# A chunked WKV kernel: six pairs loaded ahead, column sums in four column tiles of TensorE, and their copies on VectorE

## The chip, the core and the metric

The kernel runs on one core of a Trainium2 chip. The metric is the device time of one execution in microseconds (us). Every number below comes from runs of this kernel or from one profiled execution of it.

## The reference

The inputs are k and v of shape (16, 2048, 256), and two vectors w and u of 256. For each batch and channel a recurrence runs over the 2048 time steps. Cut to what matters:

```python
for t in range(seq_len):
    kk, vv = k[b, t], v[b, t]
    ww = u + kk
    qq = maximum(pp, ww)
    e1, e2 = exp(pp - qq), exp(ww - qq)
    output[b, t] = (e1 * aa + e2 * vv) / (e1 * bb + e2 + 1e-08)
    ww = pp - w + kk
    qq = maximum(ww, kk)
    e1, e2 = exp(ww - qq), exp(kk - qq)
    aa, bb, pp = e1 * aa + e2 * vv, e1 * bb + e2, qq
```

So an output is a weighted mean of the earlier v, with weights that are exponentials of k and of the distance in time, plus a weight with u for the current step.

## The kernel before, in words

**Tiling.** Time is cut into a head of 32 steps and 16 chunks ("steps", c = 0 to 15) of 126. Time lies on the partitions. The unit of work is a pair: 126 time rows of four batches, held as two tiles of 512 columns (two batches by 256 channels each). A step has four pairs. With the two pairs of the head (placed as pairs 2 and 3) there are 66 pairs.

**What is done with a pair n.**
- `load` (L111) brings k into a tile `kr` (float32) and v into `vr` (converted to bfloat16 by the transfer). `AHEAD` buffers of each exist, and the loop loads pair n + AHEAD in slot n. The k of pairs 0 and 1 and of the head is issued on SyncE's queue, all else on GpSimd's, which also writes the outputs.
- `round_k` (L283, VectorE) casts k into `km`. `logs` (L292, TensorE) makes the logarithms of two sets of weights by four matmuls with the matrices `NLE` and `NLZ` into PSUM `X`. From pair 8 on there is one `X`, of four banks.
- `exps` (L313, ScalarE) takes the exponentials of `X` into `ez` (bfloat16). `times_v` (L324, VectorE) multiplies them by v into the other half of `ez`.
- `sums` (L348, TensorE) adds up the weights and the weighted v over each half of the chunk: four matmuls of 512 columns with the one-hot matrices `OHE` and `OHV` (48 columns wide), all accumulated over the four pairs of a step into one PSUM tile `tot` of 48 rows.
- Ten slots later `den` and `num` (L500, L521, TensorE) form denominators and numerators, four matmuls each. `log_den` and `invert` (L509, L516, ScalarE) take Ln and Exp(-x), `mult` (L531, VectorE) multiplies, and `store` writes the output. PSUM holds one buffer of two banks for `den` and one of one bank for `num`.

**What is done once a step.** `copy_sums` (L366, ScalarE) copies `tot` into `ts`; `turn_sums` (L371, TensorE) transposes it by four matmuls with `Ir`; `split_sums` (VectorE) copies the result into `tsum`. Some 15 tiny operations on VectorE and ScalarE (`state_*`, `inject_*`, `carr*`) carry the state to the next step; `turn_carries` transposes it, and `inject` copies it to `row` and sends it by SyncE's DMAs into two rows of `ez`.

**The order.** `K` (L35) pins the order of each engine to the order of the program text, so the loop at L613 is the schedule. Slot n runs, in text order: load; `a3`; exps(n); `d0`; round_k(n+1); `p0`; num of tile 0 of pair n-12; `d1`; `a0`; `p1`; invert of pair n-11; `a2`; den and log_den of pair n-10; mult of tile 0; `d2`; `d3`; logs(n+1); num of tile 1; `p3`; times_v(n); sums(n); `p2`; `d4`; mult of tile 1 and store; `d5`; `p4`; `a1`. Each name in code marks is a place for small work. `PLANS` (L571) puts each small function in a place of a slot, counted from the last pair of its step: "steady" for c = 1 to 13, "before" for 14, "last" for 15.

In the steady plan `copy_sums` stands in slot 1 at `a0`, right after exps; the second half of the state (`state_add` 1 and `state_decay` 1) stands in slot 5 at `d2` and `d4`, after `inject` at `d0`. Slot 5 of a step is slot 1 of the next.

Of the kernel before, what the change touches and what calls it, by code (L numbers as in the profile page):

```python
# [22 lines left out]
def kernel(  # L23
# [35 lines left out]
    NH = NG * GB  # L59
    AHEAD = 4  # L60
    LAG = 10
    HALVES = 8
    RS = 2.0 ** -43
# [32 lines left out]
    def is_head(n):  # L96
        return pairs[n][0] < 0
# [5 lines left out]
    def tiles_of(n):  # L103
        return 1 if pairs[n] == (-1, 1) else 2
# [6 lines left out]
    def load(n):  # L111
        kr = kpool.tile([128, 4, Dm], F32, tag="kr", name="kr")
        vr = vpool.tile([128, 4, Dm], BF16, tag="vr", name="vr")
        kr_of[n], vr_of[n] = kr, vr
        c, p = pairs[n]
        if is_head(n):
            if p == 1:
                K(POOL.memset(kr[64:96, 0:2, :], 0.0))
                K(POOL.memset(vr[64:96, 0:2, :], 0.0))
            for t, x, eng in ((kr, k, SP), (vr, v, POOL)):  # L120
                for g in range(NG):
                    b = 6 * g + 4 * p
                    e = min(b + 2 * tiles_of(n), B)
                    if b < e:
                        K(eng.dma_start(out=t[g * GB:(g + 1) * GB, 0:e - b, :],  # L125
                                        in_=x[b:e, 0:T0, :].rearrange("n t d -> t n d")))
        else:
            t0 = T0 + c * TC
            r = min(128, T - t0)
            K((SP if n < 2 else POOL).dma_start(  # L130
                out=kr[0:r, :, :], in_=k[4 * p:4 * p + 4, t0:t0 + r, :].rearrange("n t d -> t n d")))
            if n >= 2:
                load_v(n)


    def load_v(n):
        c, p = pairs[n]
# [19 lines left out]
    def matrix(name, dt, width=128):  # L157
        return consts.tile([128, width], dt, tag=name, name=name)
# [10 lines left out]
    Ir = consts.tile([48, 48], F32R, tag="Ir", name="Ir")  # L169
# [31 lines left out]
    def step_matrices(E, Z, rows, N, io):  # L201
# [15 lines left out]
    OHE, OHV, OHhE, OHhV = [matrix(x, BF16, 56) for x in ("OHE", "OHV", "OHhE", "OHhV")]  # L217

    unit(0, NH)
    unit(1, NH + 1)  # L220
# [3 lines left out]
    K(POOL.memset(OHhV, 0.0))  # L224
    for g in range(NG):
        K(POOL.memset(OHhE[g * GB:(g + 1) * GB, 8 + 3 * g:9 + 3 * g], 1.0))
        K(POOL.memset(OHhV[g * GB:(g + 1) * GB, 24 + 3 * g:25 + 3 * g], 1.0))
        select(OHhE[:, 40 + 3 * g:41 + 3 * g], NE, 1.0, NH + g, -1, 1, 0)
    for n in range(2, AHEAD):
        load(n)  # L230
    kms = [consts.tile([128, 4, Dm], F32R, tag=f"km{j}", name=f"km{j}") for j in range(2)]
    for t in kms:
        K(SC.activation(t[96:128, :, :], row_of(96, 128), ACT.Copy))
# [3 lines left out]
        K(SC.activation(t[96:98, :, :], row_of(96, 98), ACT.Copy))  # L237

    def matrices_for_sums():
        K(DVE.tensor_copy(Ir, I1[0:48, 0:48]))  # L240
        for t, x in ((OHE, 8), (OHV, 24)):
            fill(t, 0.0)
            fill(t[0:HS, x:x + 1], 1.0)
            K(DVE.tensor_single_scalar(t[:, x + 8:x + 9], cc[:, 4:5], 2.0, op=ALU.mult))
        K(DVE.tensor_copy(OHE[:, 40:49:8], cc[:, 2:4]))

    def matrices_for_head():
        step_matrices(NLEh, NLZh, 0, NH, IOh)
# [60 lines left out]
    def ez_of(n):  # L309
        j = 2 * (n % 2)  # L310
        return EZ[n // 2][:, :, j:j + tiles_of(n), :]
# [20 lines left out]

    TOT, SUMS = {}, {}

    def step_of(n):
# [10 lines left out]
    def sums(n):  # L348
        c = step_of(n)
        head = c < 0  # L350
        if n == first_of[c]:
            TOT[c] = psn.tile([128, D], F32, tag="num", name="num")[0:48] if head else pst.tile(
                [48, D], F32, tag="tot", name="tot")
# [12 lines left out]
    def copy_sums(c):  # L366
        ts = small.tile([48, D], F32R, tag="ts", name="ts")
        K(SC.activation(ts, TOT.pop(c), ACT.Copy))  # L368
        st[c, "ts"] = ts

    def turn_sums(c):  # L371
# [192 lines left out]
    def at(slot, where, f, *args):  # L564
        later.setdefault((slot, where), []).append((f, args))

    def small_work(n, where):
        for f, args in later.pop((n, where), []):
# [135 lines left out]
```

## Time and profile before

| what | value |
|---|---|
| median of 4 runs | 298.59 us (297.81 to 299.89) |
| the profiled execution's own time | 297.94 us |
| its span, first to last instruction | 296.2 us |
| TensorE busy | 267.5 us (90%) |
| ScalarE busy | 270.0 us (91%) |
| VectorE busy | 247.7 us (84%) |
| GpSimd busy | 161.6 us (55%) |
| granted TensorE clock | 0.99 |

The profiled execution took 1.7 us more than its span, and it lies 0.65 us under the median. Three engines are busy most of the time, so the shares alone do not say which one sets the pace; that has to be read slot by slot. From about 66 us to 247 us the slots repeat with a period of four.

### The profile page before, as it was taken

How to read it: one execution, taken by the hardware profiler on the slowest of the kernel's cores; microseconds unless marked ns; L12 is line 12 of the kernel's file. 1: busy time of each engine (PE TensorE's matmuls, PEld its weight loads, DVE VectorE, ACT ScalarE, POOL GpSimd, SP SyncE). 2: the span in 40 equal slices, each digit the busy share in tenths (PEclk: the TensorE clock that was granted, in tenths of full speed). 3: DMA queues.
4: the chain of work that ended last, by engine and by line, in shares of the span. 5: the costliest groups of instructions: out<-in, count | busy, mean ns of one | idle time of the engine just before them, and what ended most of it. 6: DMA issues, size and time to landing. Idle time of an engine off the chain costs nothing.

```text
span 296.2 us, 3949 instructions
## 1 busy us (share of the span) xinstructions
PE 267.5 (90%) x1132; PEld 123.9 (42%) x1132; DVE 247.7 (84%) x501; ACT 270.0 (91%) x312; POOL 161.6 (55%) x231
## 2 busy tenths in 40 slices
PE   1778699899999999999999999999999999898970
PEld 0334344344444444544444444444454444333420
DVE  4778768969899989898999989998989899778660
ACT  6666799799999999999999999999999999898990
POOL 8866348736564656656465656465665654222531
PEclk9999999999999999999999999999999999999995
DMA  5999999999999999999999999999999999845876
GB/s 180 208 232 305 233 262 205 281 293 302 295 322 326 327 337 336 331 325 326 328 331 339 332 327 324 318 332 339 332 326 318 318 304 297 243 146 199 283 259 182
DMA packets 58485, 85.94 MB, mean 290 GB/s; under 512 B 6834, under 2 KB 42406, under 8 KB 58464
## 3 DMA queue, kind: packets, MB, share of 16 engines
q0 software_dynamic: 52896, 82.78, 103.4%
q1 hardware_dynamic: 5536, 2.89, 4.1%
q8 instruction: 9, 0.15, 0.2%
q14 instruction: 12, 0.10, 0.1%
q10 hardware_dynamic: 32, 0.02, 0.0%
HBM read 68.12 MB, written 34.05 MB: 345 GB/s over the span
## 4 chain that ended last, share of the span: by engine, by line
PE 39%; ACT 32%; DVE 10%; issue 8%; DMA 5%; POOL 4%; ACTq 0%; POOLq 0%; DVEq 0%
ACT ez L322 12%; PE num L527 10%; PE X L306 10%; PE den L505 9%; ACT rd L514 9%; PE tot L359 8%; ACT rd L519 7%; DMA kr<-in_k_dram 5%; DVE ez L329 4%; DVE rd L535 3%; PE den L375 2%; ACT ts L368 1%; POOL vr L140 1%; DVE km L290 1%; POOL vr L125 1%
## 5 line engine op out<-in xcount | busy, mean ns | idle before, releaser
L322 ACT ACTIVATE ez<-X 128x2048 bf16<-128x2048 f32 x58 | 109.0, 1878 | 3.0 <-PE X L306 1.2
L535 DVE TENSOR_TENSOR rd<-num,rd 128x512 f32<-128x512 f32 (+2 forms) x131 | 88.8, 685 | 13.2 <-PE num L527 7.2
L140 POOL DMA_DIRECT2D vr<-in_v_dram x64 | 50.1, 783 | 80.7 <-DVE AB L443 29.5
L329 DVE TENSOR_TENSOR ez<-ez,vr 126x2048 bf16<-126x2048 bf16 (+1 forms) x66 | 79.8, 1210 | 4.1 <-ACT ez L320 2.0
L555 POOL DMA_DIRECT2D out_dram<-rd x63 | 52.6, 835 | 45.7 <-issue 16.4
L519 ACT ACTIVATE rd<-rd 128x1024 f32<-128x1024 f32 (+3 forms) x67 | 69.7, 1041 | 0.3
L514 ACT ACTIVATE rd<-den 128x1024 f32<-128x1024 f32 (+3 forms) x67 | 67.1, 1001 | 2.7 <-PE den L505 2.5
L306 PE MATMUL X<-km,NLE 128*128 128x512 f32 x128 | 51.7, 486 | 13.5 <-DVE km L290 9.5
L290 DVE CAST km<-kr 126x1024 fp32r<-126x1024 f32 x64 | 50.8, 794 | 2.9 <-DMA kr<-in_k_dram 2.9
L527 PE MATMUL num<-ez,LfN 128*128 128x512 bf16 x128 | 49.2, 384 | 2.2 <-DVE rd L535 0.8
L527 PE MATMUL num<-ez,IdN 126*128 126x512 bf16 (+1 forms) x131 | 49.8, 381 | 0.0
L130 POOL DMA_DIRECT2D kr<-in_k_dram x62 | 48.2, 777 | 0.2 <-issue 0.2
L306 PE MATMUL X<-km,NLZ 128*128 128x512 f32 x128 | 40.5, 398 | 0.0
L359 PE MATMUL tot<-ez,OHV 126*48 126x512 bf16 x128 | 38.2, 379 | 1.8 <-DVE ez L329 1.7
L359 PE MATMUL tot<-ez,OHE 128*48 128x512 bf16 x128 | 39.2, 388 | 0.0
L505 PE MATMUL den<-ez,Id 126*128 126x512 bf16 (+1 forms) x131 | 39.1, 378 | 0.0
L505 PE MATMUL den<-ez,Lf 128*128 128x512 bf16 x128 | 38.0, 377 | 0.8 <-DVE tsum L382 0.4
L306 PEld LDWEIGHTS X<-km,NLE 128*128 128x128 f32 x128 | 23.6, 192 | 26.2 <-DVE km L290 6.6
L306 PEld LDWEIGHTS X<-km,NLZ 128*128 128x128 f32 x128 | 24.4, 192 | 6.0 <-ACT ez L320 0.4
L527 PEld LDWEIGHTS <-LfN 128*128 128x128 bf16 x128 | 12.3, 96 | 28.5 <-issue 25.4
L359 PEld LDWEIGHTS <-OHV 126*48 126x48 bf16 x128 | 13.3, 104 | 17.0 <-issue 3.3
L505 PEld LDWEIGHTS <-Lf 128*128 128x128 bf16 x128 | 12.3, 98 | 18.4 <-issue 7.3
(103 smaller groups left out, 190.5 us busy)
## 6 DMA issues: line engine op xcount, KB each, us to landing
out_dram<-rd POOLq DMA_DIRECT2D x60, 512.0 KB, 7.4
kr<-in_k_dram POOLq DMA_DIRECT2D x58, 512.0 KB, 8.1
vr<-in_v_dram POOLq DMA_DIRECT2D x60, 256.0 KB, 7.1
kr<-in_k_dram POOLq DMA_DIRECT2D x4, 504.0 KB, 10.2
kr<-in_k_dram SPq DMA_DIRECT2D x2, 512.0 KB, 5.2
ez<-row SPq DMA_DIRECT2D x64, 8.0 KB, 5.9
vr<-in_v_dram POOLq DMA_DIRECT2D x4, 252.0 KB, 9.2
out_dram<-rd POOLq DMA_DIRECT2D x2, 504.0 KB, 4.4
```

The source lines that it names most:

```text
L140: K(POOL.dma_start(out=vr_of[n][0:r, :, :], in_=v[4 * p:4 * p + 4, t0:t0 + r, :].rearrange("n t d -> t n d")))
L290: K(DVE.tensor_copy(KM[n][0:r, 0:i, :], kr_of.pop(n)[0:r, 0:i, :]))
L306: K(PE.matmul(X[q][:, i, :], m[0:kr, :], km[0:kr, i, :], start=True, stop=True))
L322: K(SC.activation(ez_of(n)[:, 0:4:2], X[2][:, :, 0:i, :], ACT.Exp))
L329: K(DVE.tensor_mul(ez[0:r, 1:4:2], ez[0:r, 0:4:2], vb[0:r].unsqueeze(1).broadcast_to([r, 2, i, D])))
L359: K(PE.matmul(TOT[c], m[0:r, :], ez_of(n)[0:r, q, i, :], start=n == first_of[c] and i == 0 and q == 0, stop=n == last_of[c] and i == tiles ...
L505: K(PE.matmul(d[:, i, :], m[0:r, :], ez_of(n)[0:r, q, i, :], start=q == 0, stop=q == 2, skip_group_check=True))
L514: K(SC.activation(RD[n][0:r, a:b, :], DEN[n][0:r, a:b, :], ACT.Ln, scale=RS))
L519: K(SC.activation(RD[n][0:r, a:b, :], RD[n][0:r, a:b, :], ACT.Exp, scale=-1.0))
L527: K(PE.matmul(d, m[0:r, :], ez_of(n)[0:r, q, i, :], start=q == 1, stop=q == 3, skip_group_check=True))
L535: K(DVE.tensor_mul(RD[n][0:r, i, :], NUM.pop((n, i))[0:r, :], RD[n][0:r, i, :]))
L555: K(eng.dma_start(out=out[4 * p + a:4 * p + b, t0:t0 + r, :].rearrange("n t d -> t n d"), in_=o[0:r, a:b, :]))
```

## The change

1. `AHEAD` goes from 4 to 6. The k of the first six pairs is issued on SyncE ahead of the loop; before, the k of pairs 4 and 5 was issued on GpSimd in the loop. The v of pairs 2 to 5 is issued by GpSimd ahead of the loop. The head's k is loaded group by group in another order, and the two zero fills of the head's tiles move from GpSimd to VectorE.
2. Twelve matmuls of 512 columns on a tile of zeros are put at TensorE's start.
3. `sums` writes four row groups of a 128-row `tot`, one for each combination of weights or weighted v and tile, each by its own column tile of TensorE; the one-hot matrices are 32 columns wide. `Ir` becomes 128 rows, and adds the groups up in the transpose.
4. `copy_sums` copies 128 rows; for c = 1 to 14 it moves from ScalarE at `a0` to VectorE at `d1` of the same slot. In the steady plan `state_add` 1 and `state_decay` 1 move from slot 5 to slot 4, at `d1` and `d2`.

```diff
-    AHEAD = 4
+    AHEAD = 6
...
-            K((SP if n < 2 else POOL).dma_start(
+            K((SP if n < AHEAD else POOL).dma_start(
                 out=kr[0:r, :, :], in_=k[4 * p:4 * p + 4, t0:t0 + r, :].rearrange("n t d -> t n d")))
-            if n >= 2:
+            if n >= AHEAD:
                 load_v(n)
...
-    for n in range(2):
+    for n in range(AHEAD):
         load(n)
...
+    zeros = consts.tile([128, D], BF16, tag="zeros", name="zeros")
+    fill(zeros, 0.0)
+    idle = psn.tile([128, D], F32, tag="num", name="idle")
+    for i in range(12):
+        K(PE.matmul(idle, zeros[:, 0:128], zeros, start=True, stop=True))
+
+    for x in (kr_of, vr_of):
+        fill(x[3][64:96, 0:2, :], 0.0)
...
     for n in range(2, AHEAD):
-        load(n)
+        load_v(n)
...
-        K(DVE.tensor_copy(Ir, I1[0:48, 0:48]))
+        K(DVE.tensor_add(Ir[:, 0:16], I1[:, 0:16], I1[:, 32:48]))
+        K(DVE.tensor_add(Ir[:, 16:32], I1[:, 64:80], I1[:, 96:112]))
+        K(DVE.tensor_add(Ir[:, 32:48], I1[:, 16:32], I1[:, 48:64]))
...
-                m = ((OHE, OHV), (OHhE, OHhV))[head][q][:, 8 - x:56 - x]
+                m = ((OHE, OHV), (OHhE, OHhV))[head][q][:, 8 - x:40 - x]
...
-                K(PE.matmul(TOT[c], m[0:r, :], ez_of(n)[0:r, q, i, :],
-                            start=n == first_of[c] and i == 0 and q == 0,
-                            stop=n == last_of[c] and i == tiles_of(n) - 1 and q == 1,
-                            skip_group_check=True))
+                y = 32 * (2 * q + i)
+                K(PE.matmul(TOT[c][y:y + 32], m[0:r, :], ez_of(n)[0:r, q, i, :],
+                            start=n == first_of[c], stop=n == last_of[c] or (head and i == 1),
+                            tile_position=(0, y), skip_group_check=True))
...
-    def copy_sums(c):
-        ts = small.tile([48, D], F32R, tag="ts", name="ts")
-        K(SC.activation(ts, TOT.pop(c), ACT.Copy))
+    def copy_sums(c, eng=SC):
+        ts = small.tile([128, D], F32R, tag="ts", name="ts")
+        if eng is SC:
+            K(SC.activation(ts, TOT.pop(c), ACT.Copy))
+        else:
+            K(DVE.tensor_copy(ts, TOT.pop(c)))
...
-                   (4, "d4", carry_weights), (4, "d5", carries), (4, "p4", turn_carries), (5, "d0", inject),
-                   (5, "d2", state_add, 1), (5, "d4", state_decay, 1)),
+                   (4, "d1", state_add, 1), (4, "d2", state_decay, 1),
+                   (4, "d4", carry_weights), (4, "d5", carries), (4, "p4", turn_carries), (5, "d0", inject)),
...
+            if f is copy_sums and 0 < c < NST - 1:
+                where, args = "d1", (DVE,)
             at(last_of[c] + slot, where, f, c, *args)
```

More of the change, by code (lines that the diff above doesn't have):

```diff
@@ L116, in load @@
         if is_head(n):
[L117 to L126, printed above, removed]
+            load_head(n, SP, kr, k)
         else:
@@ L129, in load, with load_head @@
             r = min(128, T - t0)
-            K((SP if n < 2 else POOL).dma_start(
+            K((SP if n < AHEAD else POOL).dma_start(
                 out=kr[0:r, :, :], in_=k[4 * p:4 * p + 4, t0:t0 + r, :].rearrange("n t d -> t n d")))
-            if n >= 2:
+            if n >= AHEAD:
                 load_v(n)
+    def load_head(n, eng, t, x):
+        p = pairs[n][1]
+        for g in (0, 2, 1):
+            b = 6 * g + 4 * p
+            e = min(b + 2 * tiles_of(n), B)
+            if b < e:
+                K(eng.dma_start(out=t[g * GB:(g + 1) * GB, 0:e - b, :],
+                                in_=x[b:e, 0:T0, :].rearrange("n t d -> t n d")))
     def load_v(n):
+        if is_head(n):
+            load_head(n, POOL, vr_of[n], v)
+            return
         c, p = pairs[n]
@@ L167, in fill @@
         K(DVE.memset(ap.bitcast(F32) if ap.dtype == F32R else ap, value))
-    Ir = consts.tile([48, 48], F32R, tag="Ir", name="Ir")
+    Ir = consts.tile([128, 48], F32R, tag="Ir", name="Ir")
     M1, I1, IO, IOh = [matrix(x, F32) for x in ("M1", "I1", "IO", "IOh")]
@@ L215 @@
     K(DVE.scalar_tensor_tensor(NLE[:, TC + 1:128], cc[:, 2:3], -0.5 * HS, cc[:, 4:5], ALU.mult, ALU.add))
-    OHE, OHV, OHhE, OHhV = [matrix(x, BF16, 56) for x in ("OHE", "OHV", "OHhE", "OHhV")]
+    OHE, OHV, OHhE, OHhV = [matrix(x, BF16, 40) for x in ("OHE", "OHV", "OHhE", "OHhV")]
     unit(0, NH)
@@ L226 @@
         K(POOL.memset(OHhE[g * GB:(g + 1) * GB, 8 + 3 * g:9 + 3 * g], 1.0))
-        K(POOL.memset(OHhV[g * GB:(g + 1) * GB, 24 + 3 * g:25 + 3 * g], 1.0))
-        select(OHhE[:, 40 + 3 * g:41 + 3 * g], NE, 1.0, NH + g, -1, 1, 0)
+        K(POOL.memset(OHhV[g * GB:(g + 1) * GB, 8 + 3 * g:9 + 3 * g], 1.0))
+        select(OHhE[:, 24 + 3 * g:25 + 3 * g], NE, 1.0, NH + g, -1, 1, 0)
     for n in range(2, AHEAD):
-        load(n)
+        load_v(n)
     kms = [consts.tile([128, 4, Dm], F32R, tag=f"km{j}", name=f"km{j}") for j in range(2)]
@@ L239, in matrices_for_sums @@
     def matrices_for_sums():
-        K(DVE.tensor_copy(Ir, I1[0:48, 0:48]))
-        for t, x in ((OHE, 8), (OHV, 24)):
+        K(DVE.tensor_add(Ir[:, 0:16], I1[:, 0:16], I1[:, 32:48]))
+        K(DVE.tensor_add(Ir[:, 16:32], I1[:, 64:80], I1[:, 96:112]))
+        K(DVE.tensor_add(Ir[:, 32:48], I1[:, 16:32], I1[:, 48:64]))
+        for t in (OHE, OHV):
             fill(t, 0.0)
-            fill(t[0:HS, x:x + 1], 1.0)
-            K(DVE.tensor_single_scalar(t[:, x + 8:x + 9], cc[:, 4:5], 2.0, op=ALU.mult))
-        K(DVE.tensor_copy(OHE[:, 40:49:8], cc[:, 2:4]))
+            fill(t[0:HS, 8:9], 1.0)
+            K(DVE.tensor_single_scalar(t[:, 16:17], cc[:, 4:5], 2.0, op=ALU.mult))
+        K(DVE.tensor_copy(OHE[:, 24:33:8], cc[:, 2:4]))
     def matrices_for_head():
@@ L351, in sums @@
         if n == first_of[c]:
-            TOT[c] = psn.tile([128, D], F32, tag="num", name="num")[0:48] if head else pst.tile(
-                [48, D], F32, tag="tot", name="tot")
+            TOT[c] = (psn if head else pst).tile([128, D], F32, tag="num" if head else "tot", name="tot")
         for q in range(2):
```

## The prediction

> **What bounds the kernel now.** I read the engine shares first, then the windows of the stretch that repeats, then the order on ScalarE and VectorE in one period of four slots.
>
> ```profile
> PE 267.5 (90%) x1132; PEld 123.9 (42%) x1132; DVE 247.7 (84%) x501; ACT 270.0 (91%) x312; POOL 161.6 (55%) x231
> ```
>
> ```profile
> 144.44:176.61 32.17, 31.99 (x140) 15.01 (x138) 29.49 (x57) 31.84 (x37) 18.72 (x25) 1.00 1.17 330
> ```
>
> The second line covers two periods: 32.17 us, in which TensorE (first) shows 31.99, VectorE (third) 29.49, ScalarE (fourth) 31.84. TensorE's figure is swollen, since matmuls overlap in the records. ScalarE is idle 0.33 us in 32. The period is 16.08 us, 4.02 a slot.
>
> ```profile
> 150.72 1.89 ACT L322 ACTIVATE ez<-X 128x2048 bf16<-128x2048 f32 x1
> 152.48 0.59 ACT L368 ACTIVATE ts<-tot 48x512 fp32r<-48x512 f32 x1
> 152.96 1.07 ACT L519 ACTIVATE rd<-rd 128x1024 f32<-128x1024 f32 x1
> 153.91 1.02 ACT L514 ACTIVATE rd<-den 128x1024 f32<-128x1024 f32 x1
> 154.81 1.88 ACT L322 ACTIVATE ez<-X 128x2048 bf16<-128x2048 f32 x1
> 156.57 1.07 ACT L519 ACTIVATE rd<-rd 128x1024 f32<-128x1024 f32 x1
> 157.51 0.27 ACT L394 ACTIVATE lf<-tsum 128x64 f32<-128x64 f32 x1
> 157.66 1.03 ACT L514 ACTIVATE rd<-den 128x1024 f32<-128x1024 f32 x1
> 158.90 1.88 ACT L322 ACTIVATE ez<-X 128x2048 bf16<-128x2048 f32 x1 [0.21 <-PE num L527]
> ```
>
> Each starts where the last ends, less some 0.1 us of overlap: ScalarE sets the pace. The copy of the sums holds it for 152.96 - 152.48 = 0.48 us. The only idle time is 0.21 us once a period, for `X` from TensorE, which in that slot ran four transposes of the sums (0.55 us) before num and den. So TensorE is just behind: in the chain of waits its slot is den 0.87, X 0.93, num twice 0.45, tot 0.98, plus about 0.2 a slot for the transposes and the gaps, some 3.9 of 4.02.
>
> VectorE's waits in 112 to 241 us, eight periods (total us, times, longest):
>
> ```profile
> DVE S L399 <- ACT lf L394: 4.1, 8, 0.6
> DVE rd L535 <- PE num L527: 3.2, 14, 0.2
> DVE row L477 <- PE den L472: 2.6, 8, 0.3
> DVE rd L535 <- DMA vr<-in_v_dram: 0.5, 2, 0.2
> ```
>
> That is 1.3 us a period, so VectorE works 14.7 of 16.08. No load is waited for (the 0.5 stands at `rd`, which reads no v).
>
> Startup, first VectorE, then TensorE:
>
> ```profile
> 11.30 1.23 DVE L329 TENSOR_TENSOR ez<-ez,vr 126x2048 bf16<-126x2048 bf16 x1 [0.63 <-ACT ez L320]
> 12.44 0.68 DVE L290 CAST kmh<-kr 96x1024 fp32r<-96x1024 f32 x1
> 20.16 0.69 DVE L290 CAST km<-kr 126x1024 fp32r<-126x1024 f32 x1 [0.96 <-DMA kr<-in_k_dram]
> ```
>
> ```profile
> 6.62 1.22 PE L306 MATMUL X<-km,NLE 128*128 128x512 f32 x2 [6.62 <-DVE km L290]
> 13.27 0.70 PE L306 MATMUL X<-kmh,NLEh 98*128 98x512 f32 x2
> ```
>
> The first exps ended long before 11.30, so `times_v` of pair 0 really waited for v, issued at 3.30; the cast for pair 2 is queued behind it. Pair 5's k, issued at 13.56, is waited for at 20.16.
>
> **What the skill says.** (1) "TensorEngine Tiling (Array Packing)", Key Properties: tiles work independently, but a change of tiling mode drains TensorE. Nothing in the trace of before shows a tile mode. (2) "TensorE: Matmul & The Clock Gate", Measured speedup vs the span model: three column tiles of 512 columns ran 2.38 times as fast. Not shown here either. (3) The same page, Part 1: TensorE starts at half clock until it has been busy some 3.4 us. The trace agrees: two matmuls took 1.22 us at 6.62 and 0.70 at 13.27. (4) "DMA: Bandwidth & Descriptors", Issuing engines are not separate DMA queues: transfers of all issuers share 16 engines. The trace agrees so far as the v of pair 0, 256 KB, took 7.9 us beside SyncE's k.
>
> **The change, part by part.**
>
> *Copy off ScalarE* (c = 1 to 14): -0.48 us a period there, and the 0.21 wait can go with it. ScalarE's floor becomes 16.08 - 0.48 - 0.16 = 15.44.
>
> *Copy on VectorE.* No row shows it. Nearest are the mult, 512 columns from PSUM, which starts every 0.60 us (152.56 to 153.16), and the copy of 192 columns, 0.36 us. Bounds 0.53 to 0.75; I take 0.60. VectorE then works 14.74 + 0.60 = 15.34. The wait at `row` for the transposed carries (0.32) stays, since nothing stands between `carries` and `inject`; the waits at `S` (0.5) and for num (0.4) are lead over ScalarE and TensorE, which a fuller VectorE does not have. Floor 15.34 + 0.32 = 15.66. The copy stands at `d1`, and behind it are queued mult of tile 0 (on which num of tile 1 waits), times_v, and the mult of tile 1. In that slot times_v starts 0.81 us after exps ended (153.29 against 152.48). With 0.60 added and the 0.13 of the moved state_add taken off it starts 1.28 after; TensorE's weighted sums and transposes come 0.47 later, which the shorter `tot` gives back.
>
> *Moved state_add and state_decay*: the same two instructions (0.13 and 0.14 us of VectorE's order) one slot earlier, where VectorE idles 0.23 for num. Zero; without that cover +0.27 in one slot, -0.27 in the next.
>
> *Column tiles.* 64 groups of four matmuls. At 2.38 a group goes from 0.98 to 0.41. A drain into and out of the mode: a lone matmul is recorded at 0.38 against 0.22 between starts, so up to 0.16 each. Best 0.33, serial with two drains 4 x 0.22 + 0.32 = 1.2; I take 0.6, so TensorE needs 3.9 - 0.4 = 3.5 a slot and leaves the path. In the repeating slots this alone is worth only the 0.16 a period already counted. In the last two loaded slots, where the chain runs through TensorE, it gives 2 x 0.3 = 0.6.
>
> *The period* becomes the larger floor, 15.66: -0.42. Of 13 periods between the copies of c = 1 and 14, the first one and a half are still filling (ScalarE idles 1.9 us in 50 to 58). 11.5 x 0.42 = **-4.8 us**. Ends: 0, if the late times_v returns all; 13 x 0.64 = -8.3 at ScalarE's floor.
>
> *Idle matmuls.* 12 x 0.43 = 5.2 us from about 1.3, over before the first X at 6.62. They save 0.5 us on the first X, but exps of pair 2 (at 14.01) hang on the v of pair 0. Zero; -0.5 if that v comes sooner.
>
> *Loads.* SyncE gets two more issues of about 0.65 us; behind them stand only `inject`'s DMAs, after 34 us. GpSimd loses two issues of 0.8 and two fills of 0.52. The v of pair 0 keeps its place and its rival on the engines. K of pairs 4 and 5 is asked for some 6 us earlier, so the wait of 0.96 goes; but it now competes with the v of pair 1, which landed 0.8 us before use. I take **-1.0**, ends -3 (the later loads that were just in time move up too) and +1.
>
> *VectorE at the start.* Three fills (bounded by 0.5 each) lie in its idle 1.12 us before 2.10, where it waits for GpSimd's `IO`. The three adds for `Ir` instead of a cast of 0.26 add about 0.3, inside the 0.84 that it waits for the first k. Zero; +0.5 without cover.
>
> *Depth in the loop.* 1.28 MB a slot at 3.92 us is 338 GB/s against 330 now; half-microsecond windows reach 399, but the page's best slice is 339. K has 2 to 3 us to spare, and two pairs more give 8. Zero; up to +4 if 336 is the ceiling.
>
> Sum: -4.8 - 0.6 - 1.0 = -6.4. 296.2 - 6.4 + 1.7 = 291.5 against the profiled execution's 297.94. That lies 0.65 under the median, so **292.1** as a median.
>
> **Rivals.**
> 1. *VectorE takes it back*: the late times_v and its own waits leave the period at 15.95 or more. 11.5 x 0.13 = 1.5, plus the startup's 1.0: 296. For it: VectorE would be 98% full. Against: the waits are lead.
> 2. *The transfers become the bound* at 336 GB/s: a slot of 3.95, so 46 x 0.07 = -3.2 and -1.0: 294.4. For it: the DMA share never falls below 1. Against: no load was late.
> 3. *The tile mode slows TensorE* (slower): if the four run serially with a drain on each side, a group takes 1.2, and TensorE's slot goes from 3.9 to 4.12. It decides from a group of 1.1 us on. 56 slots x 0.1 = +5.6, less 1.0: 303. For it: two changes of mode a slot. Against: the tiles have separate output rows.
> 4. *No effect*: the schedule is pinned, so the copies do move; only the startup part could come to nothing.
>
> **How the numbers follow.** Forecast 0.64, rival 1 0.15, rival 2 0.10, rival 3 0.11. The forecast spans 287 (ScalarE's floor and startup -2) to 295.5; with rivals 1 and 2 up to 297.5. About 0.5%, 1.5 us, is what a measurement of this kernel can tell from no change. Faster: the forecast, rival 2 and half of rival 1, 0.82; within: 0.07; slower: rival 3, 0.11.
>
> **What would show it.** Right: tot groups under 0.7 us; the period 15.5 to 15.8; no L368-like copy on ScalarE for c = 1 to 14; VectorE's waits for `lf` and num shrunk, that for `den` at `row` still 0.3; the k of pair 5 not waited for, v of pair 0 still landing near 11. Wrong: exps waiting for X longer than 0.2 a period (TensorE or a late cast of k), waits for kr or for stores in the loop, or tot groups over 1 us.

## The result, and the profile after

The changed kernel has a median of 297.83 us; the kernel before, run beside it, 299.14. The ratio is 0.9953, with a 95% interval of 0.9936 to 0.997. So the change saves about 1.4 us (0.0047 x 299.14), where 6.4 were forecast. The profiled execution took 298.67 us with a span of 296.9: 0.84 over its median, while the profile of before (297.94) lies 1.2 under its own. The two profiles alone would say "slower by 0.7", and only the many runs show the sign. The profiles serve here to tell where time goes, not how much the whole is. A few executions of every kernel are some per cent slower, whatever the kernel; the ratios leave them out, the medians beside them do not.

The page's engine shares and the granted clock in forty slices, of the kernel after:

```profile
PE 250.0 (84%) x1144; PEld 114.0 (38%) x1144; DVE 252.9 (85%) x520; ACT 265.0 (89%) x298; POOL 161.7 (54%) x227
PEclk9859779999999999999999999999999999999997
```

TensorE lost 17.5 us of busy time and ScalarE 5.0, and VectorE gained 5.2: the work moved as planned. The clock line is new. Before, all slices but the last showed a 9; now four slices in the first 45 us are below. (A record of the clock begins with its first change. In the profile of before that is at 10.34 us, and up to there its matmuls ran at half speed too: 1.22 us a pair at 6.62.)

The window of two periods, from the start of the exps of one pair to that of the eighth after it:

```profile
136.96:168.90 31.94, 28.73 (x140) 13.25 (x138) 30.09 (x59) 31.14 (x35) 19.50 (x25) 1.00 1.17 331
```

The period went from 16.08 us to 15.97, where 15.66 was forecast. And now no engine is full. VectorE (third figure) works 30.09 of 31.94; ScalarE (fourth) idles 0.80 us in these two periods, against 0.33 before.

Where ScalarE idles shows in its order over the slot of the copy and the next one:

```profile
152.94 1.89 ACT L339 ACTIVATE ez<-X 128x2048 bf16<-128x2048 f32 x1
154.69 1.08 ACT L539 ACTIVATE rd<-rd 128x1024 f32<-128x1024 f32 x1
155.65 1.04 ACT L534 ACTIVATE rd<-den 128x1024 f32<-128x1024 f32 x1
156.55 1.91 ACT L339 ACTIVATE ez<-X 128x2048 bf16<-128x2048 f32 x1
158.30 1.09 ACT L539 ACTIVATE rd<-rd 128x1024 f32<-128x1024 f32 x1
159.25 0.29 ACT L414 ACTIVATE lf<-tsum 128x64 f32<-128x64 f32 x1
159.58 1.03 ACT L534 ACTIVATE rd<-den 128x1024 f32<-128x1024 f32 x1
160.97 1.88 ACT L339 ACTIVATE ez<-X 128x2048 bf16<-128x2048 f32 x1 [0.36 <-PE num L547]
```

From exps to exps, the slot of the copy takes 156.55 - 152.94 = 3.61 us (4.09 before): the 0.48 is saved in full. The next slot takes 160.97 - 156.55 = 4.42 (4.09 before) and gives 0.33 back, in two places. `log_den` (L534) starts 3.03 after these exps, at 159.58, where it started 2.85 after them before: it has to wait for `den`. And the wait for `X` is 0.36, where it was 0.21. The bracket names num, whose records lie between the end of `X` and this start; of TensorE's results exps reads only `X`.

VectorE and then TensorE in the same stretch tell why:

```profile
154.58 0.68 DVE L388 CAST ts<-tot 128x512 fp32r<-128x512 f32 x1
155.18 0.68 DVE L555 TENSOR_TENSOR rd<-num,rd 128x512 f32<-128x512 f32 x1
155.78 1.22 DVE L346 TENSOR_TENSOR ez<-ez,vr 126x2048 bf16<-126x2048 bf16 x1
156.91 0.68 DVE L555 TENSOR_TENSOR rd<-num,rd 128x512 f32<-128x512 f32 x1
157.51 0.68 DVE L307 CAST km<-kr 126x1024 fp32r<-126x1024 f32 x1
158.11 0.35 DVE L402 COPY tsum<-den 128x192 f32<-128x192 f32 x1
```

```profile
156.46 0.40 PE L377 MATMUL tot<-ez,OHE 128*32 128x512 bf16 x2
157.05 0.39 PE L377 MATMUL tot<-ez,OHV 126*32 126x512 bf16 x2 [0.20 <-DVE ez L346]
157.37 0.62 PE L395 MATMUL den<-Ir,ts 128*128 128x48 f32 x4
...
158.52 0.59 PE L525 MATMUL den<-ez,Lf 128*128 128x512 bf16 x2
...
159.19 0.82 PE L323 MATMUL X<-km,NLE 128*128 128x512 f32 x2
```

The same operations before the change, where the exps of the two slots start at 150.72 and 154.81:

```profile
153.29 1.22 DVE L329 TENSOR_TENSOR ez<-ez,vr 126x2048 bf16<-126x2048 bf16 x1
...
156.06 0.36 DVE L382 COPY tsum<-den 128x192 f32<-128x192 f32 x1
```

```profile
155.40 0.62 PE L375 MATMUL den<-Ir,ts 48*128 48x48 f32 x4
...
156.47 0.59 PE L505 MATMUL den<-ez,Lf 128*128 128x512 bf16 x2
```

Read it as one chain. The copy delays times_v to 155.78, which is 2.84 after the exps of its slot (2.57 before). The weighted sums wait for it until 157.05. The transposes of `turn_sums` stand behind the sums in TensorE's order, at 157.37, 0.82 after the next exps (0.59 before). So of the 0.27 that times_v is late, the shorter sums win back 0.04. The transposes write the banks of `den`, of which there is one buffer. `split_sums` frees that buffer at 158.46: it starts at 158.11, 0.12 after the transposes end, behind the mult and the cast of k on VectorE. So the den of the next pair starts at 158.52, 1.97 after exps (1.66 before), `X` behind it at 159.19, and ScalarE gets it at 160.97.

VectorE's and ScalarE's waits in 112 to 240 us (total us, times, longest) changed as follows:

```profile
ACT ez L339 <- PE num L547: 2.8, 8, 0.4
DVE S L419 <- ACT lf L414: 2.7, 8, 0.4
DVE row L497 <- PE den L492: 2.6, 8, 0.3
...
DVE rd L555 <- PE num L547: 0.8, 5, 0.2
```

VectorE's waits at `S` and for num shrank, that at `row` stayed: as foreseen. The first line is a part of the price: ScalarE waits 0.35 us a period for `X`, where it waited 0.13 (1.0 in all before, five times); the late `log_den` is the rest.

Last, by starts of the exps: slot 10 begins at 43.31 us (40.13 before). Slots 10 to 62 take 205.42 us (207.04), and from there to the end 48.17 (49.03). That is +3.2 at the start, -1.6 in the loop, -0.9 in the tail. So two things have to be explained: the period, and the start.

### The profile page after: what moved, and what is told of

Its sections match the earlier page's. It is cut to its first block, busy times and chain, and to the rows that moved or that the text cites. A ratio compares the mean times of both kernels' runs of the same rounds, so it can differ in the third digit from the quotient of the medians.

```text
span 296.9 us, 3976 instructions
## 1 busy us (share of the span) xinstructions
PE 250.0 (84%) x1144; PEld 114.0 (38%) x1144; DVE 252.9 (85%) x520; ACT 265.0 (89%) x298; POOL 161.7 (54%) x227
## 4 chain that ended last, share of the span: by engine, by line
DVE 28%; ACT 23%; PE 20%; issue 13%; DMA 13%; POOL 1%; POOLq 0%; ACTq 0%; DVEq 0%
DMA vr<-in_v_dram 10%; ACT ez L339 9%; DVE ez L346 9%; DVE rd L555 8%; ACT rd L534 7%; PE X L323 6%; PE num L547 5%; PE den L525 5%; ACT rd L539 3%; DVE km L307 3%; DMA out_dram<-rd 3%; PE tot L377 2%; DVE ts L388 2%; PE den L395 1%; ACT ez L337 1%
## 5 line engine op out<-in xcount | busy, mean ns | idle before, releaser
L144 POOL DMA_DIRECT2D vr<-in_v_dram x64 | 54.3, 848 | 74.3 <-DVE ez L346 22.1
L575 POOL DMA_DIRECT2D out_dram<-rd x63 | 51.4, 816 | 48.9 <-issue 18.6
L534 ACT ACTIVATE rd<-den 128x1024 f32<-128x1024 f32 (+3 forms) x67 | 67.3, 1005 | 4.3 <-PE den L525 3.8
L323 PE MATMUL X<-km,NLE 128*128 128x512 f32 x128 | 49.9, 472 | 8.6 <-DVE km L307 3.0
L307 DVE CAST km<-kr 126x1024 fp32r<-126x1024 f32 x64 | 47.9, 749 | 1.8 <-DMA kr<-in_k_dram 1.8
L122 POOL DMA_DIRECT2D kr<-in_k_dram x60 | 46.5, 775 | 3.3 <-issue 2.6
L323 PE MATMUL X<-km,NLZ 128*128 128x512 f32 x128 | 41.7, 408 | 0.1
L377 PE MATMUL tot<-ez,OHV 126*32 126x512 bf16 x128 | 26.0, 397 | 6.5 <-DVE ez L346 6.3
L323 PEld LDWEIGHTS X<-km,NLE 128*128 128x128 f32 x128 | 21.2, 194 | 26.3 <-ACT ez L339 14.8
L377 PE MATMUL tot<-ez,OHE 128*32 128x512 bf16 x128 | 25.8, 399 | 0.0
L337 ACT ACTIVATE ez<-X 128x1024 bf16<-128x1024 f32 (+1 forms) x16 | 14.7, 966 | 7.3 <-PE X L323 7.2
```

Source lines behind the costliest of these rows:

```text
L144: K(POOL.dma_start(out=vr_of[n][0:r, :, :], in_=v[4 * p:4 * p + 4, t0:t0 + r, :].rearrange("n t d -> t n d")))
L307: K(DVE.tensor_copy(KM[n][0:r, 0:i, :], kr_of.pop(n)[0:r, 0:i, :]))
L323: K(PE.matmul(X[q][:, i, :], m[0:kr, :], km[0:kr, i, :], start=True, stop=True))
L377: K(PE.matmul(TOT[c][y:y + 32], m[0:r, :], ez_of(n)[0:r, q, i, :], start=n == first_of[c], stop=n == last_of[c] or (head and i == 1), tile ...
L534: K(SC.activation(RD[n][0:r, a:b, :], DEN[n][0:r, a:b, :], ACT.Ln, scale=RS))
L575: K(eng.dma_start(out=out[4 * p + a:4 * p + b, t0:t0 + r, :].rearrange("n t d -> t n d"), in_=o[0:r, a:b, :]))
```

## Experiments

**Theory A (period).** The `den` buffer, held by the late transposes, keeps TensorE's chain to `X` long. Transposes that run ahead of the sums should bring 15.66. Rivals: VectorE is simply too full, or the tiles cost TensorE time. **Theory B (start).** The short sums leave TensorE too little to do, and its clock falls. Rival: the six early k delay the v.

### The period

**Transposes early** (e1). The transposes stand one place earlier, ahead of the sums of their slot, and the split after that slot's second mult:

```diff
-        "steady": ((1, "a0", copy_sums), (1, "p2", turn_sums), (2, "d1", split_sums), (2, "a2", state_logs),
+        "steady": ((1, "a0", copy_sums), (1, "p3", turn_sums), (1, "d5", split_sums), (2, "a2", state_logs),
```

> The changed kernel, with the transposes of the sums put before the sums of the slot instead of after them, and the copy of their result one place earlier (steady plan only). No operation is added or removed. Theory 'den bank': the transposes hold the only den buffer, so den of the next slot, X and exps wait for the copy on VectorE, the late times_v, the weighted sums, the transposes and the copy out. Then the period falls from 15.95 to 15.4-15.6 us and the slot of 4.41 us to about 3.9; in all 4 to 5 us. Rival 'VectorE is full' (15.1 of 16 busy): VectorE has the same work, so the period stays at 15.8 to 15.95 and the time within 1 us.

Measured: 295.24 us, ratio 0.9836 (0.9785 to 0.9888); period 15.69. TensorE, and then ScalarE, of this kernel:

```profile
154.88 0.62 PE L395 MATMUL den<-Ir,ts 128*128 128x48 f32 x4
155.44 0.40 PE L377 MATMUL tot<-ez,OHE 128*32 128x512 bf16 x2
...
156.32 0.59 PE L525 MATMUL den<-ez,Lf 128*128 128x512 bf16 x2
```

```profile
154.69 1.91 ACT L339 ACTIVATE ez<-X 128x2048 bf16<-128x2048 f32 x1
...
158.77 1.88 ACT L339 ACTIVATE ez<-X 128x2048 bf16<-128x2048 f32 x1 [0.17 <-PE num L547]
```

The transposes no longer wait for the weighted sums, den comes 1.63 us after exps began (1.97 in the kernel after), and the slot is 4.08 instead of 4.42. VectorE does the same work in both, so the rival "VectorE is simply too full" is out. The run moves the transposes and the split together; which of the two moves counts more, no run here tells.

**Copy back on ScalarE** (e4):

```diff
-            if f is copy_sums and 0 < c < NST - 1:
-                where, args = "d1", (DVE,)
```

> The changed kernel with the copies of the sums back on ScalarE, right after exps. ScalarE has 0.48 us a period more, VectorE 0.6 less. Theory 'den bank': the copy is early again, so the slot after it loses its waits (4.41 to 3.8-3.9 us) and the slot of the copy goes from 3.61 to 4.09: period 15.8 to 15.9, the time within 1 us of the changed kernel; the move of the copy was worth nearly nothing. Rival 'moving the copy brought the whole gain': period back to 16.08.

Measured: 298.51 us, 0.9965 (0.9943 to 0.9987); period 15.99, with slots of 4.10, 3.96, 3.95 and 4.00. That is neither of the two numbers expected. Against the 15.96 of the kernel after (a mean over six periods) the move of the copy alone is worth 0.03 a period: what it takes off ScalarE in one slot comes back in the next.

**No column tiles** (e7): `sums`, `OHE`, `OHV`, `Ir` and `ts` back at 48 rows, without tiles; the copy stays on VectorE.

```diff
...
-                m = ((OHE, OHV), (OHhE, OHhV))[head][q][:, 8 - x:40 - x]
+                m = ((OHE, OHV), (OHhE, OHhV))[head][q][:, 8 - x:56 - x]
...
```

> The changed kernel without the column tiles: sums as before (48 rows, 0.98 us a group), copies on VectorE. Theory 'den bank': the copy on VectorE delays times_v and with it the sums of weighted v by 0.47 us, and the sums are 0.6 longer again, so the slot after the copy grows to 4.9 or more and the period to 16.2-16.5, longer than before; the tiles are what pays for the move of the copy. Rival 'VectorE full': the period is set by VectorE and stays at 15.95. Clock 0.98 or more if the shorter sums cause its fall.

Measured: 299.15 us, 0.9991 (0.9964 to 1.0019); period 16.07, between the two numbers expected. The tiles are worth 0.11 a period when the transposes are late and the copy is on VectorE.

**No column tiles, transposes early** (e11): the edits of e1 and e7 together.

```diff
...
-                m = ((OHE, OHV), (OHhE, OHhV))[head][q][:, 8 - x:40 - x]
+                m = ((OHE, OHV), (OHhE, OHhV))[head][q][:, 8 - x:56 - x]
...
-        "steady": ((1, "a0", copy_sums), (1, "p2", turn_sums), (2, "d1", split_sums), (2, "a2", state_logs),
+        "steady": ((1, "a0", copy_sums), (1, "p3", turn_sums), (1, "d5", split_sums), (2, "a2", state_logs),
```

> The changed kernel with early transposes, but sums without the column tiles (no filling matmuls are needed then). If the early transposes alone freed the path, the period is 15.7 and the time 293 to 295. If TensorE's slot counts as well (3.9 us with the long sums against ScalarE's 3.87), the period is 15.85 to 16.0 and the time 296 to 298: then the tiles pay in the loop only together with the early transposes.

Measured: 299.50 us, 1.0005 (0.9982 to 1.0028); period 16.16. Neither expectation was met. ScalarE, slot after the copy:

```profile
159.87 1.03 ACT L532 ACTIVATE rd<-den 128x1024 f32<-128x1024 f32 x1 [0.24 <-PE den L523]
161.25 1.88 ACT L336 ACTIVATE ez<-X 128x2048 bf16<-128x2048 f32 x1 [0.35 <-PE num L545]
```

It waits twice for TensorE, 0.59 us. Here the bank is not what holds: in the mean of these slots the split has freed it 1.29 us after exps, and den starts only at 2.17. The early transposes push the long sums back in TensorE's order, and den stands behind them. The four cases of the period, copy on VectorE, as means over six periods, are:

| | transposes late | transposes early |
|---|---|---|
| sums untiled | 16.07 | 16.16 |
| sums tiled | 15.96 | 15.69 |

Each edit alone gives -0.11 or +0.09; both give -0.38. They are two parts of one path.

Two more runs split the 0.11 by which the changed kernel is below the 16.07 of before (means over six periods again). With the copy on ScalarE, the tiles alone (e5, below) have 16.06, and e4 has 15.99. In the loop e4 differs from e5 in the depth, which is worth nothing there (e2 has 15.96 like the kernel after), and in the place of `state_add` 1 and `state_decay` 1. So the tiles brought 0.01, the moved state operations 0.07 and the moved copy 0.03. It fits the same chain: in e5 `state_add` stands ahead of times_v in the slot of the copy.

### The start

**Only the loads and the idle matmuls** (e6): sums untiled, copy on ScalarE, small operations as before; `AHEAD = 6`, the early k and the idle matmuls stay.

```diff
...
-                y = 32 * (2 * q + i)
-                K(PE.matmul(TOT[c][y:y + 32], m[0:r, :], ez_of(n)[0:r, q, i, :],
...
+                K(PE.matmul(TOT[c], m[0:r, :], ez_of(n)[0:r, q, i, :],
...
-            if f is copy_sums and 0 < c < NST - 1:
-                where, args = "d1", (DVE,)
...
```

> Of the change only the loads (AHEAD 6, k of the first six pairs on SyncE, v of pairs 2 to 5 ahead of the loop, the fills on VectorE) and the twelve idle matmuls; sums and copies as before. Theory 'clock by shorter sums': the sums are long again, the clock stays at 0.98 or more, slot 9 starts at 35.5 to 37.5, period 16.08. Rival 'the loads cause it': half clock after 13 us, slot 9 at 38 or later. v of pair 1 lands at 13 to 15 us in both (12.3 before).

Measured: 298.71 us, 0.9985 (0.9953 to 1.0018). Slot 9 starts at 36.33 (36.93 before): -0.6. The k of pair 5 is not waited for, v of pair 1 lands at 13.57 (12.25 before), and the clock is full from 4.55 us until the tail. In this profile the loads bring a small gain, and they do not make the start late.

Six profiles can be compared here. Up to slot 9 the kernel after, e1 and e4 run one and the same program, and e6, e7 and e11 run another, which has the same loads and idle matmuls and differs by the tiles. The tiled ones reach slot 9 at 40.11, 39.81 and 38.31, the untiled ones at 36.33, 37.07 and 38.48. So profiles of one program differ by 2 us, and the tiles put slot 9 back by 2.1 in the mean. The clock is plainer: in all their runs it is 0.936 to 0.967 with tiles (64 runs) and 0.968 to 0.992 without (50).

**Only the tiles** (e5): `AHEAD = 4`, no idle matmuls, copy on ScalarE, `state_add` 1 and `state_decay` 1 where they were. (The fills and the order of the head's loads stay as in the kernel after.)

```diff
-    AHEAD = 6
+    AHEAD = 4
...
-    for i in range(12):
+    for i in range(0):
...
```

> Of the change only the column tiles: AHEAD 4, no idle matmuls at the start, the copies on ScalarE, state_add 1 and state_decay 1 in slot 5 as before. Theory 'clock': the shorter sums leave TensorE less busy between 10 and 35 us, so that it falls to half clock there, which the kernel before never did; slot 9 starts at 38.3 or later instead of 36.9, and the mean granted clock is under 0.97. Rival 'the loads cause it' (v that lands late leaves TensorE idle): clock as before, 0.985 to 0.99, slot 9 at 36.9 or earlier. Period: 15.95 to 16.0 (TensorE 0.6 a slot shorter, ScalarE's floor 15.92 with the copy on it), so the tiles alone bring at most the 0.1-0.15 that ScalarE waited.

Measured: 299.84 us, 1.0000 (0.9975 to 1.0025); slot 9 at 40.13, period 16.06. The first line is of e5, the second of e6, the same pair of matmuls:

```profile
24.22 1.20 PE L323 MATMUL X<-km,NLE 128*128 128x512 f32 x2
```

```profile
23.39 0.70 PE L320 MATMUL X<-km,NLE 128*128 128x512 f32 x2 [0.30 <-DVE km L304]
```

With tiles and no idle matmuls TensorE runs at half speed until 39.8 us. In this profile the tiles alone make a delay as long as that of the kernel after. (The clock line of e5's page says full speed there, since the record begins only with the first change, at 39.8 us; the durations contradict it.) It is an extreme profile: a record of 0.988 or more, which leaves out so long a stretch, stands in 4 of the 22 runs of e5; the other 18 have 0.942 to 0.980.

**Four ahead** (e2), on top of the kernel after:

```diff
-    AHEAD = 6
+    AHEAD = 4
```

> The changed kernel with AHEAD back at 4: the k of pairs 4 and 5 is issued by GpSimd in the loop again. Theory 'late v': v of pair 0 lands near 11.2 us instead of 12.3 and v of pair 1 near 12.3 instead of 15.1; exps of pair 2 start near 14.0 instead of 15.5, and the half-clock stretch after 13 us goes, since TensorE no longer idles 3.4 us. Slot 16 starts some 1.5 to 2.5 us earlier; period unchanged at 15.95. Rival 'the other parts of the change make the start late' (fills on VectorE, column tiles): v still lands at 12 us or later, or exps of pair 2 stay at 15.5.

Measured: 298.61 us, 0.9954 (0.9929 to 0.9978), as the kernel after. V of pair 1 lands at 12.54, so it is early again, yet slot 9 starts at 38.93, within the 38.31 to 40.11 of the three profiles above, with half clock from 13.2 to 23.5 us and from 30.3 to 40.5 us. The expectation that the first of these stretches goes was missed. The rival "early k delay v" is not the cause of the slow start.

**Zero matmuls in three more places** (e3): 12 in slot 0, 6 in slot 6, 8 in slot 7.

```diff
...
+    for n, where, count in ((0, "p3", 12), (6, "p2", 6), (7, "p2", 8)):
+        at(n, where, keep_busy, count)
```

> The changed kernel with 26 more matmuls of zeros that nothing reads, where TensorE idles at the start: 12 in slot 0 before its sums, 6 in slot 6, 8 in slot 7. Theory 'clock': the two stretches at half clock (13 to 23 us and 33 to 40 us) go, X of pairs 2 to 5 takes 1.1 us instead of 2.1, den and X of slot 8 take 1.8 instead of 3.6, so that slot 9 starts at about 37.5 instead of 40.1, and the time falls by 1.5 to 3 us. Rival 'the slow matmuls lie beside waits for v': the clock is full and slot 9 still starts within 0.7 us of 40.1.

Measured: 297.87 us, 0.9952 (0.9924 to 0.9981); the clock rose to 0.966 in the median, but slot 9 still starts at 39.32. Half clock stood from 20.2 to 33.8, from behind the first place into the second, and the eight matmuls of slot 7 stood ahead of the transposed carries, so that `row` came late:

```profile
36.98 0.29 DVE L497 CAST row<-den 128x128 bf16<-128x128 f32 x1 [1.31 <-PE den L492]
```

A miss: too few places, and one on the path.

**Early transposes and two filler matmuls a slot** (e8), on top of e1:

```diff
...
+    for n in range(0, 9):
+        at(n, "p2", keep_busy, n)
```

`keep_busy` runs two matmuls of zeros, 128 columns wide.

> The changed kernel with the transposes early, as in the run that moved them, and two matmuls of zeros after the sums of each of slots 0 to 8 (0.43 us a slot, about what the column tiles took off). Theory 'clock': the half-clock stretches before 41 us go or shrink, slot 9 starts at 36 to 38 instead of 39.8, and with the period of 15.7 the time is 292.5 to 294. Rival 'the clock does not depend on such matmuls, or TensorE is not on the path there': slot 9 stays at 39 to 40, the time at 295.2.

Measured: 293.69 us, 0.9803 (0.9747 to 0.9858); slot 9 at 36.75 in its profile (39.81 in e1), clock 0.976 in the median (0.951). Windows of 14 to 22 us and 30 to 38 us, first of the kernel after, then of e8 (the third figure from the right is the clock, the fourth busy figure ScalarE):

```profile
14.00:22.00 8.00, 7.82 (x22) 3.42 (x20) 5.46 (x11) 4.29 (x6) 6.22 (x8) 0.50 1.29 256
30.00:38.00 8.00, 5.34 (x23) 2.35 (x21) 5.91 (x16) 4.88 (x8) 3.36 (x4) 0.72 1.24 306
```

```profile
14.00:22.00 8.00, 7.32 (x30) 2.97 (x30) 6.40 (x12) 6.15 (x9) 6.78 (x9) 0.82 1.30 275
30.00:38.00 8.00, 6.85 (x26) 3.20 (x27) 5.39 (x12) 5.65 (x8) 3.57 (x4) 0.79 1.26 303
```

At clock 0.50 TensorE shows 7.82 of 8 us busy with 22 matmuls and ScalarE gets 4.29 us of work; with eight matmuls more to run, at 0.82, TensorE is less busy and ScalarE gets 6.15. Useless work made the start faster. Against e1 the medians differ by 1.5 us and the intervals overlap, so the 3 us between the two profiles (e8's is the fastest of its six runs) are the larger end of its worth.

**The same fillers, a quarter as wide** (e13):

```diff
-            K(PE.matmul(d, zeros[:, 0:128], zeros, start=True, stop=True))
+            K(PE.matmul(d[0:32], zeros[:, 0:32], zeros, start=True, stop=True, tile_position=(0, 0)))
```

> The version with early transposes and two filler matmuls a slot at the start, but each filler is 32 columns wide (one column tile) instead of 128; its duration stays the same. If the clock follows how long TensorE is busy, the narrow fillers keep it up as the wide ones did: mean granted clock about 0.97, slot 9 near 36.8, time 293 to 294.5. If it follows how much of the array works, a narrow filler counts a quarter: clock about 0.95, slot 9 near 39.8, time about 295.2 as without fillers.

Measured: 294.47 us, 0.9839 (0.978 to 0.9899); clock 0.970 in the median, slot 9 at 39.10 in its profile, whose clock in the two windows is 0.72 and 0.64. That lies between the two answers: the mean clock is near the first, slot 9 near the second. In these four runs narrow fillers give most of the mean clock back, which speaks for busy time; that width counts too is not excluded.

**Without the twelve idle matmuls** (e10), on top of e8:

```diff
-    for i in range(12):
+    for i in range(0):
```

> The version with early transposes and two filling matmuls a slot, without the twelve idle matmuls at TensorE's start. As the prediction had it (worth nothing, since exps of pair 2 hang on v): the first X takes 2.3 us instead of 1.3, exps of pair 2 start within 0.5 us of 13.6, the time within 0.7 us of 293.7. Theory 'clock': without them TensorE comes late to full clock or not at all before 35 us (the tiles alone never came), slot 9 starts at 38 or later and the time is 1.5 to 3 us longer.

Measured: 293.43 us, 0.9796 (0.9756 to 0.9836), against 293.69. Once TensorE is kept busy later, the twelve matmuls bring nothing that the medians show. In the profiles they do: without them the clock is full only from 18.64 us, and slot 9 starts at 38.24 in place of 36.75, as the second theory had it. The profile of e8 is its fastest run and that of e10 (293.73) a middle one, so this difference is an upper end.

**V ahead of the later k** (e9): e8, with the k and v of pairs 4 and 5 issued on GpSimd behind the v of pairs 0 to 3.

```diff
-            K((SP if n < AHEAD else POOL).dma_start(
+            K((SP if n < 2 else POOL).dma_start(
...
-    for n in range(2, AHEAD):
+    for n in range(2, 4):
         load_v(n)
+    for n in range(4, AHEAD):
+        load(n)
...
```

> The version with early transposes and two filling matmuls a slot, and the k of pairs 4 and 5 issued on GpSimd ahead of the loop, behind the v of pairs 0 to 3, instead of on SyncE. Theory 'late v': with six pairs ahead the v of pair 1 landed at 13.1 to 15.1 us in five profiles (12.3 before); now it lands near 12.3, exps of pair 3 start 0.5 us earlier, and the time falls by 0.3 to 1 us to about 293. Rival 'the transfers share the engines anyway': v of pair 1 at 13 or later, the time within 0.5 us of 293.7.

Measured: 295.81 us, 0.9885 (0.9848 to 0.9921). V of pair 1 lands at 12.38 as expected, yet the time is not better than that of e8. Its profile (292.05 us) is its fastest run and shows no cause. What the other order of the loads is worth stays open.

**Four ahead, with early transposes and fillers** (e12), on top of e8:

```diff
-    AHEAD = 6
+    AHEAD = 4
```

> The version with early transposes and two filling matmuls a slot, with AHEAD 4. If the depth matters only in the start: k of pair 5 is waited for again, slot 9 starts 0.5 to 1 us later than 36.75, the period stays 15.7 and the time is 294 to 295. If the transfers become the bound at the faster pace (338 GB/s against 330), k of some pair is waited for in the loop with four ahead, and the time is 296 or more.

Measured: 294.34 us, 0.9806 (0.9777 to 0.9835), not to be told from e8. Its profile has one long stop in the loop: two slots took 10.6 us in place of 7.9. TensorE, then VectorE:

```profile
64.39 0.59 PE L525 MATMUL den<-ez,Lf 128*128 128x512 bf16 x2 [1.40 <-DMA ez<-row]
...
65.25 1.41 PE L323 MATMUL X<-km,NLE 128*128 128x512 f32 x2
```

```profile
68.44 0.69 DVE L555 TENSOR_TENSOR rd<-num,rd 128x512 f32<-128x512 f32 x1 [2.99 <-PE num L547]
```

No load was late for its use: k of pair 17, which took 8.7 us, landed at 62.17, and its cast started at 62.26 in its turn. TensorE waited for the small transfer of `row`, issued at 56.24, which took 8.0 us (5.6 in the median of this profile), and behind that wait its clock was at half from 64.87 to 68.28. Whether the depth has a part in that slow transfer, one profile does not tell; in the medians six ahead is worth nothing that these runs show.

## Why the prediction was wrong

The sign was right and the size was not: -1.4 us against -6.4, outside the range. Step by step:

| step | forecast, us | measured, us |
|---|---|---|
| period, slots 10 to 62 | 11.5 x -0.42 = -4.8 | -1.6 (period -0.11) |
| last two loaded slots | -0.6 | -0.9 from slot 62 to the end |
| loads, at slot 9 | -1.0 | -0.6, +0.1 and +1.6 (e6, e7, e11 against before) |
| clock of TensorE, at slot 9 | 0, not priced | +2.1 (three profiles with tiles against three without) |
| start in the median | -1.0 | +1.1, what is left to -1.4 |

The rows but the last are read from profiles, and one program's profiles differ by up to 2 us at slot 9.

**The step that failed** is this: "TensorE's weighted sums and transposes come 0.47 later, which the shorter `tot` gives back". times_v came 0.27 later, not 0.47, and the shorter sums gave 0.04 of it back. The transposes come after sums that wait for times_v, so the work that the tiles shortened had to wait anyway (0.20 us at 157.05), and the next den has to wait for VectorE's split behind the transposes. The period was computed as the largest floor of any one engine. It was a path over VectorE, TensorE, the `den` banks, VectorE again, TensorE and ScalarE. The profile of before showed it: the 0.21 us for `X` once a period stood in just that slot, and I had written the transposes beside it. Taking that wait as something that goes with the copy, instead of asking what ends first once it is gone, was the error. The prediction had named the sign, exps waiting for `X` longer than 0.2 a period: it is 0.35. Experiment e1 shows the rest: with the transposes and the split out of the way, the period is 15.69.

That this is nearly the forecast's 15.66 is luck in part. The forecast had VectorE work 15.34 and wait 0.32. In e1 it works 15.00 a period (90.03 us in the six from 111.64 to 205.81) and waits 0.70, at `row` 0.33 and for `lf` 0.30, a wait that the forecast had put aside as lead. ScalarE works 15.47 there, where its floor was forecast as 15.44, so it is the nearer bound. And the moved `state_add` and `state_decay`, put at zero, brought 0.07 a period, most of what the period gained: they stood ahead of times_v, at the head of that same path.

**The second failure** was a zero. The prediction priced the tiles on TensorE's path only and the idle matmuls at nothing. It cited from the Trainium skill ("TensorE: Matmul & The Clock Gate", Part 1) that the clock is low until TensorE has been busy, but did not ask which later stage would fall under it. The same part says that the clock follows how busy TensorE has lately been, and "A second HAM failure mode: psum-queue depth-cycling" that many small gaps make it go to and fro. The traces agree, and they give numbers. TensorE at the two falls of the kernel after, and at the same wait before as at the second:

```profile
13.63 0.61 PE L377 MATMUL tot<-ez,OHV 126*32 126x512 bf16 x2 [3.36 <-DVE ez L346]
...
33.04 0.89 PE L323 MATMUL X<-km,NLE 128*128 128x512 f32 x2 [2.23 <-ACT ez L337]
```

```profile
31.49 0.72 PE L306 MATMUL X<-km,NLE 128*128 128x512 f32 x2 [1.59 <-ACT ez L320]
```

The clock fell at 12.97 and at 33.45. In all fifteen traces the changes of the clock lie on a grid: they are 3.41 us or a whole multiple of it apart (6.83, 10.24, 13.65 and so on). So take the stretches of 3.41 us between grid points and ask how much of each TensorE was busy. Ahead of the two falls it was 21% and 35%. Of 1185 stretches at full clock in the fifteen traces, 34 end in a fall, 19 of these before the tail, and all 34 were busy 60% or less; of the 1151 that kept the clock, eight were busy 51 to 60% and the rest 61% or more. In the kernel before the emptiest ahead of the tail has 61%. A group of tiled sums takes 0.4 us in place of 0.98, and the 0.58 less is 17% of a stretch. So the kernel before was only just busy enough, and the tiles took that away. What brings the clock back is less plain: in e1 three stretches that were 97 to 100% busy, from 14.27 to 24.51, did not.

Across the runs of the kernel after, the time goes with the clock: three at 0.966 and more took 295.4 to 296.1 us, two at 0.938 took 298.9 and 299.3, though the runs between scatter (297.0 to 298.7 at 0.963 and 0.964). What the clock costs in the median is not measured by itself: the start as a whole is a remainder (+1.1), and the +2.1 is of six profiles.

**Right:** the copy on VectorE takes 0.60 us (154.58 to 155.18); the wait at `row` stayed at 0.3; the k of pair 5 is not waited for, and no load is waited for in the loop. (The v of pair 0 landed at 12.26 in the profile after, later than the 11 expected; see below.) The group of four tiled sums is recorded at 0.4 us where the four may run together, its instructions starting within 0.1 us of each other (152.45 and 152.46 in one slot), so 0.6 was too cautious. No drain shows: from the last num to the first sum there are 0.31 us, as before. Rival 3 is out. The idle matmuls are worth nothing in the medians (e10).

**The rivals.** The number of rival 1 (period 15.95, 296 us) came nearest, but its reason is not the one found: VectorE is idle 0.92 us a period, and with the same work on it e1 runs at 15.69. It had the late times_v right. Rival 2 is out too: e8 moves 337 GB/s in the window of two periods (136.96 to 168.90), at a period of 15.66. (The prediction's 338 is right as 330 scaled by the periods; 1.28 MB in 3.92 us, as it has it, would be 327.)

**Open.** Why profiles of one and the same start reach slot 9 up to 2 us apart. In the profile of the kernel after the v of pairs 0 and 1 landed at 12.26 and 15.07 us, in the other kernels with these loads at 10.4 to 11.2 and 13.1 to 14.1, and its first fall came in the wait for that v; the grid of the clock also lies differently in each run, with the first rise between 4.0 and 6.8 us in the kernels with idle matmuls. Neither was tested. Open too are whether width of a matmul counts for the clock beside its time, and why e9 is not faster.

The best version is e8, or e10, which is the simpler: 293.43 us and 0.9796 of before (0.9756 to 0.9836). It beats both kernels; the interval of the kernel after begins at 0.9936.

## What to carry to other kernels

When work moves off the engine that sets the pace, do not take the next engine's sum as the new period: follow the slot's chain over the engines, and above all over a buffer that exists once, to see what ends first afterwards. A small wait in the old profile marks where that chain already touches. And where a change makes TensorE's work shorter, look for stages in which it was only just busy enough to keep its clock: saved work can cost speed there.

## What the runs showed of the hardware that was not expected

- Cutting TensorE's work in a partly idle stretch slowed everything else on it: with sums of 0.4 us in place of 0.98, matmul pairs of 0.70 us took 1.20 until 39.8 us (e5), and two useless matmuls a slot (0.6 us) shortened the stretch to slot 9 by 3 us (e8 against e1, one profile each).
- The granted clock changed only at points 3.41 us apart, and no idle time of that length was needed for a fall: it came with 2.23 us (kernel after, at 33.45) and 1.40 us (e12, at 64.87) as the longest. In these traces each fall followed a stretch of 3.41 us that was busy 60% or less.
- Four column tiles of 32 columns, 128 rows deep and 512 columns long, start within 0.1 us of each other and are recorded at 0.4 us. Going in and out of tiles left no gap to be seen.
- Twelve matmuls on zeros (5.2 us) brought TensorE's first `X` from 1.22 to 0.73 us; a few microseconds later, at 12.97, the clock was at half again.
- A transfer of 8 KB (`row`) took 8.0 us in e12, where the median is 5.6. TensorE waited 1.40 us for it, and then ran 3.41 us at half clock.
